# A hybrid block on one core: x and the first weights delivered by partition, x normalised in place behind the first projection

## The chip, the core and the metric

The kernel runs on one core of a Trainium2 chip, as one launch. The metric is the device time in microseconds (us); three runs of the kernel before took 1364.17, 1364.27 and 1365.17, the median is 1364.27.

The core has engines that work side by side, each through its own queue in order: TensorE (PE, with PEld for loading its stationary operand), VectorE (DVE), ScalarE (ACT), GpSimd (POOL), and SyncE (SP), which here only issues transfers (DMA). An instruction at the head of a queue that waits for a semaphore holds up all that stand behind it.

## The reference

The block has an RMS norm of x (512 tokens, 2048 features), one wide input projection, two mixers (a gated linear recurrence A, a sparse attention with an indexer B), gates, a merge, an output projection into the residual, and a final RMS norm. What matters here is its head:

```
h = rmsnorm(x, norm_w[layer])           # x / sqrt(mean(x^2) + 1e-6) * w, per token
proj = h @ w_in[layer]
(a_q, a_f, a_i, a_g, c_q, c_kv, k_idx_raw, w_idx_raw, b_g, m_a, m_b) = jnp.split(proj, SPLIT_POINTS, axis=-1)
...
cq = rmsnorm(c_q, q_norm_w)
k_idx = layernorm(k_idx_raw, kidx_norm_w, kidx_norm_b)
w_idx = w_idx_raw * (IDX_HEADS ** -0.5 * IDX_DIM ** -0.5)
```

The norm of x is a factor per token times a weight per feature. Since a projection is linear, the factor per token may be applied to h or to the columns of proj.

## The kernel before, in words

All large products are taken in three passes: each operand is split into a rounded high part (ACT copies it to a narrower format) and the low rest (DVE subtracts), and high x high, low x high and high x low are summed on TensorE. So `split` (L71) is one ACT and one DVE instruction, and every tile of weights costs both (`prep`, L157, fills two tiles ahead; `load`, L123, has two raw buffers, so a load waits until the low part of the tile two before it is done).

`start` (L250) is the first stage. x comes in four blocks of 128 tokens, tokens on partitions. For each block ACT squares and sums (L299), the factor per token goes onto a diagonal (L307), TensorE transposes 16 pieces of 128 x 128 (L313) and spreads the factors over partitions by a product with ones (L339), DVE multiplies by weight and factor (L350, for the first block L318 and L399), ACT takes the high part (L322) and DVE or POOL the low part (L326). The results are xh and xl, features on partitions, 16 feature tiles of 512 tokens, which every later projection reads. In between, `project` (L371) multiplies each block by the first 272 columns (256 of a_i, 16 of w_idx): 48 matmuls of 272 columns a block, 192 in all. The small vectors come as rows and are turned by one transposition (L432).

Behind it the order is that of the list `jobs` at the end: `feat_job` for kidx (L1167, 48 matmuls of 512 columns), two for cq (L1169, L1171) and one for ckv (L1173), 96 each, and then the pairs (`pair_unit`, L1096), which multiply 2 x 2 blocks of features and tokens with seven products in place of eight. The pairs need sums and differences of x: `pair_gen` (L1057) forms x again as xh + xl (L1061), takes four differences of 256 tokens (L1064 to L1067) and splits them. Such generators stand in lanes and are moved on one step by `pump` (L189), which `feat_job` calls after each column tile of each chunk of four feature tiles; `prep` comes once per chunk. The step at which a lane starts thus sets which of its instructions stand next to each other and which have a weight split between them. `kidx_gen` (L602) normalises the keys in lane "norm": two splits, two pairs of matmuls with ones (L609), one row of factors by Ln and Exp.

Of the kernel before, what the change touches and what calls it, by code (L numbers as in the profile page):

```python
# [50 lines left out]
def hybrid_block(ctx, tc, x, norm_w, w_in, lb_table, gnorm_a, q_norm_w, kv_norm_w, w_uq,  # L51
                 w_qidx, w_ukv, kidx_norm_w, kidx_norm_b, w_pa, w_pb, w_out, rel_bias,
                 final_norm_w, c_ident, c_levels, c_buckets, c_flip, out):
# [38 lines left out]
    const.tile([128, 16], F32, name="gap")  # L92
# [156 lines left out]

    def start():  # L250
        R.v0 = enter("v0")
        p0 = enter("p0", side="right")
        ident = p0.tile([128, 128], F32, name="ident")
        A.dma_start(ident, c_ident)
        HF = D // 2
        nw = p0.tile([16, 128], F32, name="nw")
        wc = p0.tile([128, 16], F32, name="wc")
        xs = [[p0.tile([128, HF], F32, name=f"x{t}{i}") for i in range(2)] for t in range(4)]
        ys = [p0.tile([128, 4, 128], F32, name=f"y{g}") for g in range(4)]
        diag = p0.tile([128, 128], F32, name="diag")  # L260
        sq = p0.tile([128, HF], mybir.dt.bfloat16, name="sq")
        st = p0.tile([128, 4, 4], F32, name="st")
        rows = p0.tile([128, 128], F32, name="rows")
        G.memset(rows, 1.0)
        G.tensor_copy(ones_r, rows)
        wh = [p0.tile([128, 4, 272], FR, name=f"fh{i}") for i in range(4)]
        wl = [p0.tile([128, 4, 272], FR, name=f"fl{i}") for i in range(4)]
        raw = [None] * 4

        def load_x(t):  # L270
            for i in range(2):
                SP.dma_start(xs[t][i], x2[t * 128:(t + 1) * 128, i * HF:(i + 1) * HF])

        def load_w(i):
            raw[i] = p0.tile([128, 4, 272], F32, name=f"fr{i}")
            for o, c0, c1 in ((0, 2048, 2304), (256, 4992, 5008)):
                SP.dma_start(raw[i][:, :, o:o + c1 - c0],
                             w_in[i * 512:(i + 1) * 512, c0:c1].rearrange("(k p) n -> p k n", p=128))

        SP.dma_start(nw, norm_w.rearrange("o (k d) -> (o k) d", d=128))  # L280
        load_x(0)
        load_w(0)
        load_w(1)
        load_x(1)
        load_w(2)
        load_w(3)
        load_x(2)
        load_x(3)
        A.activation(st[:, 0, 0:1], eps, AF.Sqrt)
        warm = bank("warm")  # L290
        for _ in range(4):
            PE.matmul(warm[:, 0:128], ones, ones, start=True, stop=True)
        G.memset(rows, 0.0)
        pw = mmp.tile([128, T], F32, name="acc")
        PE.transpose(pw[:, 0:16], nw, ident[0:16, 0:16])
        V.tensor_copy(wc, pw[:, 0:16])

        def square(t, i):
            A.activation(sq, xs[t][i], AF.Square, accum_out=st[:, t, i:i + 1])  # L299

        def rstd(t):
            V.tensor_add(st[:, t, 2:3], st[:, t, 0:1], st[:, t, 1:2])
            A.activation(st[:, t, 2:3], st[:, t, 2:3], AF.Sqrt, bias=eps, scale=1.0 / D)

        def on_diag(t):
            V.reciprocal(st[:, t, 3:4], st[:, t, 2:3])
            V.tensor_scalar(diag, ident, st[:, t, 3:4], None, op0=OP.mult)  # L307

        def turn(t, g):
            pt = bank("pt")  # L310
            for j in range(4):
                k = g * 4 + j
                PE.transpose(pt[:, j * 128:(j + 1) * 128],  # L313
                             xs[t][k // 8][:, (k % 8) * 128:(k % 8) * 128 + 128], ident)
            return pt

        def weigh(pt, g):
            V.tensor_tensor(ys[g], pt.rearrange("p (j t) -> p j t", j=4),  # L318
                            wc[:, g * 4:g * 4 + 4, None].to_broadcast([128, 4, 128]), op=OP.mult)

        def high(t, g):
            A.activation(xh[g][:, :, t * 128:t * 128 + 128], ys[g], AF.Copy)  # L322

        def low(t, g):
            o = slice(t * 128, t * 128 + 128)
            (G if t and g % 2 else V).tensor_tensor(xl[g][:, :, o], ys[g], xh[g][:, :, o].bitcast(F32),  # L326
                                                    op=OP.subtract)

        def w_high(i):
            A.activation(wh[i], raw[i], AF.Copy)  # L330

        def w_low(i, eng):
            eng.tensor_tensor(wl[i], raw[i], wh[i].bitcast(F32), op=OP.subtract)

        v = hg[0, "v"] = R.v0.tile([128, 4, 256], F32, name="hv")

        def spread():
            pr = mmp.tile([128, T], F32, name="acc")
            PE.matmul(pr[:, 0:128], ones, diag, start=True, stop=True)  # L339
            r = p0.tile([128, 128], F32, name="rrow", bufs=2)  # L340
            V.tensor_copy(r, pr[:, 0:128])
            return r
# [1231 lines left out]
```

## Time and profile before

| | |
|---|---|
| profiled execution | 1364.6 us |
| its span, first to last instruction | 1362.5 us |
| mean granted TensorE clock | 0.997 |
| instructions | 26714 |
| read from HBM | 167.89 MB, 149 GB/s with what is written |
| DMA engines, mean busy share, 47 to 125 us | 0.46 |

The profile is one execution. Its page gives busy time by engine and the chain of work that ended last, followed back from the end. The queries of the trace give groups of instructions (line, engine, operation, output <- input, shapes, count, busy time, mean duration in ns, idle time of the engine ahead of them and its releaser), timelines (start, duration, engine, line; in brackets the idle time before and its releaser), waits (line <- releaser: us in total, times, longest), and windows (busy time of each engine in a stretch, then granted clock, DMA share and GB/s).

### The profile page before, as it was taken

Reading aid. Unit: us, or ns where it says so; the run is one execution under the profiler, and the core shown is the slowest. Engines: PE = TensorE matmul, PEld = TensorE weight load, DVE = VectorE, ACT = ScalarE, POOL = GpSimd, SP = SyncE. Lnnn points to the kernel's source line nnn. Section 1 sums busy time; section 2 is a strip of 40 time slices with the busy share of each in tenths; the row PEclk is TensorE's granted clock in tenths of the full one; section 3 lists DMA queues with packets and bytes.
Section 4 is the critical chain, followed back from the end, with each engine's and each line's share of the span. In section 5 each row is a group of like instructions: output and inputs, shape, how many; then the busy total and the mean of one; then the engine's idle time right before and its main releaser. Section 6 shows DMA issues by size and latency. Waiting matters only on the chain.

```text
span 1362.5 us, 26714 instructions
## 1 busy us (share of the span) xinstructions
PE 1345.9 (99%) x10940; PEld 1250.4 (92%) x10940; DVE 1065.8 (78%) x1744; ACT 654.7 (48%) x1047; POOL 42.0 (3%) x57
## 2 busy tenths in 40 slices
PE   7999999999999999999999999999999999999997
PEld 7888999999999999999999798888888888899996
DVE  7896889998898888886777888775556658899856
ACT  5555445445554445445655353546434334354434
POOL 2100000000000000000000000020101100000000
PEclk9999999999999999999999999999999999999999
DMA  6334345544453454445334433435856556643554
GB/s 207 94 108 140 96 154 157 158 149 139 128 148 109 135 152 144 147 144 164 104 104 125 140 86 117 128 114 185 267 163 204 192 179 216 209 153 112 171 198 172
DMA packets 144156, 204.77 MB, mean 150 GB/s; under 512 B 10473, under 2 KB 85922, under 8 KB 143906
## 3 DMA queue, kind: packets, MB, share of 16 engines
q1 hardware_dynamic: 143746, 202.75, 47.6%
q8 instruction: 85, 1.39, 0.4%
q10 hardware_dynamic: 288, 0.33, 0.1%
q14 instruction: 37, 0.30, 0.1%
HBM read 167.89 MB, written 35.15 MB: 149 GB/s over the span
## 4 chain that ended last, share of the span: by engine, by line
PE 94%; DVE 3%; ACT 1%; issue 1%; DMA 0%; SPq 0%; ACTq 0%; DVEq 0%
PE pp L78 15%; PE pp L77 15%; PE pp L76 15%; PE acc L76 13%; PE acc L78 13%; PE acc L77 13%; PE hl L81 2%; PE acc L81 1%; PE ho L81 1%; PE sc L76 1%; PE sc L77 1%; PE sc L78 1%; PE pt L313 0%; PE hp L81 0%; PE po L78 0%
## 5 line engine op out<-in xcount | busy, mean ns | idle before, releaser
L150 ACT ACTIVATE bh<-wr 128x768 fp32r<-128x768 f32 x128 | 108.1, 845 | 218.3 <-issue 110.7
L152 ACT ACTIVATE wh<-sv 128x512 fp32r<-128x512 f32 x256 | 151.6, 622 | 85.6 <-DVE sv L145 66.5
L73 DVE TENSOR_TENSOR wl<-wr,wh 128x1024 fp32r<-128x1024 f32 (+1 forms) x104 | 125.7, 1209 | 61.5 <-ACT wh L72 61.2
L78 PE MATMUL pp<-sh,wl 128*128 128x256 f32 x624 | 172.8, 277 | 0.0
L76 PE MATMUL pp<-sh,wh 128*128 128x256 f32 x624 | 172.8, 277 | 0.0
L77 PE MATMUL pp<-sl,wh 128*128 128x256 f32 x624 | 172.7, 277 | 0.0
L153 DVE TENSOR_TENSOR bl<-wr,bh 128x768 fp32r<-128x768 f32 x128 | 122.3, 955 | 51.3 <-ACT bh L150 50.7
L154 DVE TENSOR_TENSOR wl<-sv,wh 128x1024 fp32r<-128x1024 f32 x128 | 156.5, 1223 | 7.3 <-ACT wh L152 1.1
L72 ACT ACTIVATE wh<-wr 128x1024 fp32r<-128x1024 f32 (+1 forms) x104 | 108.1, 1041 | 109.3 <-PE acc L77 57.5
L76 PE MATMUL acc<-xh,wh 128*128 128x512 f32 x304 | 121.4, 399 | 0.0
L78 PE MATMUL acc<-xh,wl 128*128 128x512 f32 x304 | 118.7, 390 | 0.0
L77 PE MATMUL acc<-xl,wh 128*128 128x512 f32 x304 | 118.5, 390 | 0.0
L77 PEld LDWEIGHTS pp<-sl,wh 128*128 128x128 f32 x624 | 117.4, 188 | 0.0
L78 PEld LDWEIGHTS pp<-sh,wl 128*128 128x128 f32 x624 | 117.3, 188 | 0.0
L76 PEld LDWEIGHTS pp<-sh,wh 128*128 128x128 f32 x624 | 117.3, 188 | 0.0
L78 PE MATMUL pp<-xh,bl 128*128 128x256 f32 x416 | 114.9, 276 | 0.0
L77 PE MATMUL pp<-xl,bh 128*128 128x256 f32 x416 | 114.9, 276 | 0.0
L76 PE MATMUL pp<-xh,bh 128*128 128x256 f32 x416 | 114.9, 276 | 0.0
L76 PE MATMUL acc<-yh,wh 128*128 128x512 f32 x256 | 100.2, 392 | 0.0
L78 PE MATMUL acc<-yh,wl 128*128 128x512 f32 x256 | 99.8, 390 | 0.0
L77 PE MATMUL acc<-yl,wh 128*128 128x512 f32 x256 | 99.8, 390 | 0.0
L145 DVE TENSOR_TENSOR sv<-wr 128x512 f32<-128x512 f32 x128 | 87.9, 687 | 8.5 <-DMA wr<-in_w_in_dram 6.5
(395 smaller groups left out, 3638.7 us busy)
## 6 DMA issues: line engine op xcount, KB each, us to landing
wr<-in_w_in_dram SPq DMA_DIRECT2D x136, 512.0 KB, 3.7
wr<-in_w_out_dram SPq DMA_DIRECT2D x32, 512.0 KB, 3.7
mg<-gate_d SPq DMA_DIRECT2D x48, 256.0 KB, 4.2
gate_d<-c SPq DMA_DIRECT2D x44, 256.0 KB, 5.1
wr<-in_w_in_dram SPq DMA_DIRECT2D x36, 256.0 KB, 3.0
wr<-in_w_pa_dram SPq DMA_DIRECT2D x16, 512.0 KB, 6.0
wr<-in_w_pb_dram SPq DMA_DIRECT2D x16, 512.0 KB, 4.7
x<-in_x_dram SPq DMA_DIRECT2D x8, 512.0 KB, 4.8
```

Source lines behind the costliest of these rows:

```text
L72: A.activation(hi, src, AF.Copy)
L73: V.tensor_tensor(lo, src, hi.bitcast(F32), op=OP.subtract)
L76: PE.matmul(ps, lh, rh, start=first, stop=False, skip_group_check=True)
L77: PE.matmul(ps, lh, rl, start=False, stop=False, skip_group_check=True)
L78: PE.matmul(ps, ll, rh, start=False, stop=last, skip_group_check=True)
L81: PE.matmul(ps, l, r, start=first, stop=last, skip_group_check=True)
L145: V.tensor_tensor(sv[:, 0:2, :], b[:, 1:3, :], b[:, 0:1, :].to_broadcast([128, 2, 256]), op=OP.add)
L150: A.activation(bh, b[:, 1:4, :], AF.Copy)
L152: A.activation(vh[:, i:i + 2, :], sv[:, i:i + 2, :], AF.Copy)
L153: V.tensor_tensor(bl, b[:, 1:4, :], bh.bitcast(F32), op=OP.subtract)
L154: V.tensor_tensor(vl, sv, vh.bitcast(F32), op=OP.subtract)
```

## The change

- The host lays out x with features on partitions (x_t), the 272 first weight columns by partition (w_first), norm_w (w_norm), and the small vectors as columns (w_cols). No transposition is left in the first stage, and no L313, L339, L350.
- The first projection takes high and low parts of x times norm_w, without the factor per token, all four token blocks together, in five chunks of 2, 2, 4, 4, 4 feature tiles. ACT takes the high parts (scale by norm_w), DVE the low parts, POOL the high parts of the weights. ACT squares x by pairs of tiles into two buffers, DVE sums them (`add`, one chunk late).
- The factor is formed behind the first chunk of kidx (`stats`), the first projection's results are scaled by it there, and it is spread over partitions behind the second (`spread`). kidx and the first cq job run on x without factor, and their evacuations (now on DVE) multiply by it.
- x is normalised in place on DVE (`normal`) behind kidx and in the first cq job, where xh and xl are also split anew (`renew`). `pair_gen` reads this x, without the addition, and enters its lane after the first cq job in place of before kidx.

```diff
-            A.activation(xh[g][:, :, t * 128:t * 128 + 128], ys[g], AF.Copy)
...
+        parts = ((0, 2), (2, 4), (4, 8), (8, 12), (12, 16))
...
+        def square(k):
+            squares[k] = p0.tile([128, 2, T], F32, name="sq", bufs=2)
+            A.activation(squares[k], R.xt[k], AF.Square)
+
+        def add(k):
+            if k:
+                V.tensor_tensor(sums, squares.pop(0) if k == 1 else sums, squares.pop(k), op=OP.add)
...
+        for c, (k0, k1) in enumerate(parts):
+            n = slice(0, k1 - k0)
+            wh.append(p0.tile([128, 4, 272], FR, name="fh", bufs=3))
+            wl.append(p0.tile([128, 4, 272], FR, name="fl", bufs=3))
+            G.tensor_copy(wh[c][:, n], wr[c][:, n])
+            for k in range(k0, k1):
+                src = R.xt[k // 2][:, k % 2, :]
+                hi, lo = xh[k // 4][:, k % 4, :], xl[k // 4][:, k % 4, :]
+                A.activation(hi, src, AF.Copy, scale=wc[:, k:k + 1])
+                V.scalar_tensor_tensor(lo, src, wc[:, k:k + 1], hi.bitcast(F32), op0=OP.mult, op1=OP.subtract)
+            V.tensor_tensor(wl[c][:, n], wr[c][:, n], wh[c][:, n].bitcast(F32), op=OP.subtract)
+            if c < 2:
+                load_group(c + 3)
+            while behind:
+                add(behind.popleft())
+            for k in range(k0 // 2, k1 // 2):
+                square(k)
+                behind.append(k)
+            for n in range(3):
+                three(c, n)
+        load_ahead()
+        while behind:
+            add(behind.popleft())
+        V.tensor_tensor(R.total, sums[:, 0, :], sums[:, 1, :], op=OP.add)
...
+    def stats():
+        ps = bank("st")
+        for t in range(4):
+            PE.matmul(ps[:, t:t + 1], R.total[:, t * 128:t * 128 + 128], ones[:, 0:1], start=True, stop=True)
+        A.activation(R.rinv, ps[:, 0:4], AF.Sqrt, bias=eps, scale=1.0 / D)
+        V.reciprocal(R.rinv, R.rinv)
...
+    def spread():
+        ps = bank("st")
+        PE.matmul(ps, ones, R.dg[:, 128:640], start=True, stop=True)
+        A.activation(R.row, ps, AF.Copy)
+
+    def normal(k):
+        for i in range(2):
+            y = R.xt[k][:, i, :]
+            V.scalar_tensor_tensor(y, y, wc[:, 2 * k + i:2 * k + i + 1], R.row, op0=OP.mult, op1=OP.mult)
+
+    def renew(k):
+        s = slice(2 * (k % 2), 2 * (k % 2) + 2)
+        split(xh[k // 2][:, s, :], xl[k // 2][:, s, :], R.xt[k])
...
-        A.activation(R.kx[:, 0, :], ps, AF.Copy)
+        V.tensor_tensor(R.kx[:, 0, :], ps, R.row, op=OP.mult)
...
-            V.tensor_tensor(a, xh[k // 2][:, s, :].bitcast(F32), xl[k // 2][:, s, :].bitcast(F32), op=OP.add)
...
+    feat_job(w_in, 4864, 1, NK, 4, x_rhs, kx_evac,
+             after={0: stats, 1: spread, 2: lambda: normal(0), 3: lambda: (normal(1), normal(2))})
+    lane("norm", kidx_gen)
+    feat_job(w_in, 4096, 2, NK, 4, x_rhs, cq_evac(0),
+             after={i: lambda i=i: ([renew(k) for k in (2 * i, 2 * i + 1)],
+                                    [normal(k) for k in ((3,), (4, 5), (6, 7), ())[i]]) for i in range(4)})
     lane("misc", pair_gen)
-    feat_job(w_in, 4864, 1, NK, 4, x_rhs, kx_evac)
-    lane("norm", kidx_gen)
-    feat_job(w_in, 4096, 2, NK, 4, x_rhs, cq_evac(0))
```

How the instructions now stand is shown at three places. Lines in rows of the changed kernel are its own.

First, ACT in the first projection: xh are the high parts, sq the squares (two buffers in turn, each read by DVE's sums), wh the high parts of kidx's weights. Before, from its second block of tokens on:

```order
L299 ACTIVATE sq_123,st_124<-x20_114 128x1024
L322 ACTIVATE xh2_90<-y2_120 128x4x128
L299 ACTIVATE sq_123,st_124<-x21_115 128x1024
L322 ACTIVATE xh2_90<-y3_121 128x4x128
L303 ACTIVATE st_124<-st_124,cols_75 128x1
```

and in the changed kernel, from chunk 2 (feature tiles 4 to 7) to kidx:

```order
L332 ACTIVATE xh1_92<-xt2_114,wc_80 128x512 x2
L332 ACTIVATE xh1_92<-xt3_117,wc_80 128x512 x2
L309 ACTIVATE sq_248<-xt2_114 128x1024
L309 ACTIVATE sq_250<-xt3_117 128x1024
L332 ACTIVATE xh2_90<-xt4_119,wc_80 128x512 x2
L332 ACTIVATE xh2_90<-xt5_121,wc_80 128x512 x2
L309 ACTIVATE sq_314<-xt4_119 128x1024
L309 ACTIVATE sq_316<-xt5_121 128x1024
L332 ACTIVATE xh2_90<-xt6_123,wc_80 128x512 x2
L332 ACTIVATE xh2_90<-xt7_125,wc_80 128x512 x2
```

Before, a square wrote a scratch tile that nobody reads and a sum beside it; now each pair of squares stands between the high parts of one chunk and those of the next, and writes a buffer that DVE must have read.

Second, DVE in `pair_gen`: sv are the differences, sl the low part of a pair's sums (it needs the high part sh, which ACT makes from sv), wl the low part of weights. Before:

```order
L1061 TENSOR_TENSOR sv_880<-xh2_90,xl2_93 128x1024
L1064 TENSOR_TENSOR sv_882<-sv_880 128x256
L1065 TENSOR_TENSOR sv_882<-sv_880 128x256
L1066 TENSOR_TENSOR sv_882<-sv_882,sv_880 128x256
L1067 TENSOR_TENSOR sv_882<-sv_882,sv_880 128x256
L73 TENSOR_TENSOR wl_888<-wr_805,wh_887 128x1024
L73 TENSOR_TENSOR sl4_907<-sv_882,sh4_906 128x1024
```

and in the changed kernel:

```order
L1005 TENSOR_TENSOR sv_819<-xt1_111 128x256
L1006 TENSOR_TENSOR sv_819<-xt1_111 128x256
L1007 TENSOR_TENSOR sv_819<-sv_819,xt1_111 128x256
L1008 TENSOR_TENSOR sv_819<-sv_819,xt1_111 128x256
L72 TENSOR_TENSOR sl1_112<-sv_819,sh1_836 128x1024
L72 TENSOR_TENSOR wl_840<-wr_772,wh_839 128x1024
```

The addition is gone, and the weight subtract that stood between the last difference and sl now stands behind sl.

Third, DVE from the middle of the first cq job on, where before there were only weights, key normalisation and pairs (nt and suml belong to the key normalisation, L622 and L605 before):

```order
L72 TENSOR_TENSOR suml_646<-nsq_619,sumh_645 128x512
L72 TENSOR_TENSOR xl1_95<-xt2_114,xh1_92 128x1024
L72 TENSOR_TENSOR xl1_95<-xt3_117,xh1_92 128x1024
L374 SCALAR_TENSOR_TENSOR xt4_119<-xt4_119,wc_80,dg6_124 128x512 x2
L374 SCALAR_TENSOR_TENSOR xt5_121<-xt5_121,wc_80,dg6_124 128x512 x2
L72 TENSOR_TENSOR wl_676<-wr_596,wh_675 128x1024
L569 SCALAR_TENSOR_TENSOR nt_617<-nt_617,cols_75,rr_664 128x512
```

The renewed low parts (xl) and the normalisations (xt, with the spread factor dg6) stand among the weights and the steps of the key normalisation, in one queue.

More of the change, by code (lines that the diff above doesn't have):

```diff
@@ L248, in x_rhs @@
         return xh[k // 4][:, k % 4, :], xl[k // 4][:, k % 4, :]
+    xs_h, xs_l = [], []
     def start():
         R.v0 = enter("v0")
+        R.x = enter("sums")
         p0 = enter("p0", side="right")
[L253 to L280, printed above, removed]
@@ L282, in start @@
+        A.dma_start(wc, w_norm)
+        load_x(0, 0)
         load_w(0)
+        load_x(0, 1)
         load_w(1)
         load_x(1)
[L285 to L291, printed above, removed]
-            PE.matmul(warm[:, 0:128], ones, ones, start=True, stop=True)
-        G.memset(rows, 0.0)
-        pw = mmp.tile([128, T], F32, name="acc")
-        PE.transpose(pw[:, 0:16], nw, ident[0:16, 0:16])
@@ L296, in start @@
[L296 to L333, printed above, removed]
-        v = hg[0, "v"] = R.v0.tile([128, 4, 256], F32, name="hv")
[L337 to L342, printed above, removed]
@@ L387, in start @@
-        pts = [turn(0, g) for g in range(4)]
-        weigh(pts[0], 0)
-        weigh(pts[1], 1)
-        square(0, 0)
-        square(0, 1)
-        rstd(0)
-        on_diag(0)
-        w_high(0)
-        weigh(pts[2], 2)
-        r = spread()
-        def scaled(g):
-            V.tensor_tensor(ys[g], ys[g], r[:, None, :].to_broadcast([128, 4, 128]), op=OP.mult)
-            high(0, g)
-        scaled(0)
-        scaled(1)
-        w_low(0, V)
-        w_high(1)
-        low(0, 0)
-        weigh(pts[3], 3)
@@ new lines, in start @@
+        load_group(2)
+        heat_src = p0.tile([128, 128], F32, name="rows")
+        G.memset(heat_src, 1.0)
+        G.tensor_copy(ones_r, heat_src)
+        A.activation(R.rinv[:, 0:1], eps, AF.Sqrt)
+        warm = mmp.tile([128, T], F32, name="acc")
+        for _ in range(8):
+            PE.matmul(warm[:, 0:128], ones, ones, start=True, stop=True)
+        pools4 = [(mmp, "acc"), (sdp, "sd")] * 2
+        accs = [pool.tile([128, T], F32, name="pf", tag=tag)[:, 0:272] for pool, tag in pools4]
@@ L1042, in open_norms @@
         R.kx = R.i.tile([128, 1, T], F32, name="kx")
-        R.x = enter("sums")
     def open_pairs():
```

147 lines of the change are left out of this document (66 added, 81 removed).

## The prediction

> **What bounds the kernel now.** I read the page first, then who waited for whom on TensorE, then the timelines of TensorE, VectorE (DVE) and ScalarE (ACT) over the first 130 us, where the whole change lies.
>
> ```profile
> PE 1345.9 (99%) x10940; PEld 1250.4 (92%) x10940; DVE 1065.8 (78%) x1744; ACT 654.7 (48%) x1047; POOL 42.0 (3%) x57
> PE 94%; DVE 3%; ACT 1%; issue 1%; DMA 0%; SPq 0%; ACTq 0%; DVEq 0%
> ```
>
> TensorE bounds it: it is busy 99% of the span and 94% of the last chain. Its waits, longest first (line, waited for, us, times):
>
> ```profile
> PE pt L313 <- DMA x<-in_x_dram: 2.3, 1, 2.3
> PE acc L81 <- ACT xh L322: 1.8, 1, 1.8
> ...
> PE hl L81 <- DVE tot L789: 0.5, 1, 0.5
> ```
>
> All but some 1.2 us of its waiting lies before 38 us. Behind that, any wait that the change brings is added to the end whole, and any work that it removes comes off whole. TensorE's timeline (start, us, what):
>
> ```profile
> 5.99 3.68 PE L313 MATMUL pt<-ident,x 128*128 128x128 f32 x16 [2.32 <-DMA x<-in_x_dram]
> 24.41 0.66 PE L81 MATMUL acc<-fh,xh 128*128 128x272 f32 x4
> 26.91 0.67 PE L81 MATMUL acc<-fl,xh 128*128 128x272 f32 x4
> 47.11 0.48 PE L76 MATMUL acc<-xh,wh 128*128 128x512 f32 x1
> 49.28 0.39 PE L76 MATMUL acc<-xh,wh 128*128 128x512 f32 x1
> 58.12 0.39 PE L76 MATMUL acc<-xh,wh 128*128 128x512 f32 x1
> 125.23 0.28 PE L76 MATMUL pp<-xh,bh 128*128 128x256 f32 x1
> ```
>
> Three marks matter: the first real work at 5.99, the first kidx matmul at 47.11 (end of the first projection), the first matmul of the pairs at 125.23. From 24.41 to 26.91 five groups of four go by, 0.125 us a matmul, so the 192 of the first projection are 24.0 us; the other 23 are loads, transpositions, the spreading of norm factors and waits. From 49.28 to 58.12 are 39 matmuls of 512 columns, 0.227 each.
>
> **The first projection after the change.** It loses 64 transpositions and the waits around them, and keeps the 192 matmuls. Rows for what feeds it (chain of waits; groups of instructions; windows with, at the end, granted clock, DMA share and GB/s):
>
> ```profile
> 1.19 4.76 DMA x<-in_x_dram
> L448 POOL CAST levels<-lev 128x192 uint8<-128x192 f32 x1 | 0.3, 342 | 585.7 <-DMA lev<-in_levels_dram 585.7
> L265 POOL CAST ones_r<-rows 128x128 fp32r<-128x128 f32 x1 | 0.3, 289 | 0.1
> L333 POOL TENSOR_TENSOR fl<-fr,fh 128x1088 fp32r<-128x1088 f32 x1 | 2.5, 2542 | 19.6 <-ACT fh L330 19.6
> L299 ACT ACTIVATE sq<-x 128x1024 bf16<-128x1024 f32 x8 | 8.4, 1045 | 3.5 <-DMA x<-in_x_dram 3.4
> L333 DVE TENSOR_TENSOR fl<-fr,fh 128x1088 fp32r<-128x1088 f32 x3 | 3.9, 1288 | 0.5 <-ACT fh L330 0.5
> L622 DVE SCALAR_TENSOR_TENSOR nt<-nt,cols,rr 128x512 f32<-128x512 f32 x1 | 0.7, 747 | 0.0
> L1487 ACT ACTIVATE o<-o,rfin x4: 722/724/725, 1345.7 to 1356.8; 128x512 f32<-128x512 f32 x4
> 8.00:10.00 2.00, 2.00 (x10) 1.61 (x8) 1.60 (x5) 1.67 (x4) 0.00 (x0) 1.00 1.15 355
> 10.00:12.00 2.00, 0.27 (x2) 0.08 (x1) 1.86 (x5) 0.80 (x3) 0.00 (x0) 1.00 1.02 394
> 12.00:14.00 2.00, 0.98 (x5) 0.77 (x6) 2.00 (x3) 2.00 (x3) 0.00 (x0) 0.84 1.14 338
> 14.00:16.00 2.00, 2.00 (x10) 2.00 (x11) 2.00 (x4) 1.26 (x3) 0.00 (x0) 0.50 1.17 343
> 16.00:18.00 2.00, 2.00 (x13) 1.78 (x13) 1.50 (x3) 1.83 (x3) 0.00 (x0) 0.80 1.04 412
> ```
>
> Start: the first x load took 4.76 us to land; half of it, issued 0.4 us earlier, lands at about 5.7, the first weights behind it at 6.4. POOL's cast of the weights is not in the trace at this size: two casts give 0.83 ns an element, 0.63 us for 544, its subtract 2.3 ns, 1.3 us; I take the cast, first matmul at 7.2 (7.9 by the other). Chunks 0 and 1 have 24 matmuls (3.0 us) each, chunk 2 has 48 (6.0): TensorE is through them at 19.5.
>
> Then a loop binds. There are two square buffers; the next square (ACT) needs the sum (DVE) that stands behind the chunk's weight subtract, and the next chunk's x copies stand behind the squares in ACT's queue. One turn: copy 0.72, four x subtracts of the L622 kind (0.75, next one 0.67 later) 2.68, weight subtract 1.21, sum 1.22, two squares 2.0, handing over 0.3: 8.1 us against 6.0 of TensorE. Chunk 2's last x lands at 13.7 (3.2 MB ahead of it at 0.36 MB/us), so its squares end at 20.3 and chunk 3 starts at 21.0, chunk 4 at 29.1, and kidx, whose weight copy stands behind chunk 4's squares, at 37.3. Against 47.11 that is **9.8 us gained**. Without the loop it would be 7.2 + 24.0 = 31.4, 15.7 gained; with slow casts and loads 39, 8 gained.
>
> **From kidx to the pairs.** Here work is added to DVE. Its timeline before (start, us), the windows row of the stretch, and rows for what it waits on:
>
> ```profile
> 47.11:125.23 78.12, 78.12 (x345) 64.14 (x343) 62.24 (x94) 42.90 (x55) 0.00 (x0) 1.00 0.46 132
> 54.25 0.42 DVE L1064 TENSOR_TENSOR sv<-sv 128x256 f32<-128x256 f32 x1
> 54.59 0.42 DVE L1065 TENSOR_TENSOR sv<-sv 128x256 f32<-128x256 f32 x1
> 54.92 0.42 DVE L1066 TENSOR_TENSOR sv<-sv 128x256 f32<-128x256 f32 x1
> 55.38 0.42 DVE L1067 TENSOR_TENSOR sv<-sv 128x256 f32<-128x256 f32 x1
> 55.72 1.22 DVE L73 TENSOR_TENSOR wl<-wr,wh 128x1024 fp32r<-128x1024 f32 x1
> 56.93 1.23 DVE L73 TENSOR_TENSOR sl<-sv,sh 128x1024 fp32r<-128x1024 f32 x1
> 58.07 1.22 DVE L73 TENSOR_TENSOR wl<-wr,wh 128x1024 fp32r<-128x1024 f32 x1
> 63.07 0.68 DVE L73 TENSOR_TENSOR suml<-kx,sumh 128x512 fp32r<-128x512 f32 x1
> 63.67 1.22 DVE L73 TENSOR_TENSOR sl<-sv,sh 128x1024 fp32r<-128x1024 f32 x1
> L504 ACT ACT_TABLE_LOAD x1 | 1.3, 1283 | 0.0
> wr<-in_w_in_dram SPq DMA_DIRECT2D x4, 256.0 KB, 3.0
> ```
>
> Before, DVE is busy 62 of 78 us and TensorE never waits. An operation frees DVE 0.08 us before its end: 1024 wide 1.14, 512 wide 0.60, 256 wide 0.34.
>
> The change drops eight additions (L1061, 9 us) and adds sixteen normalisations (16 x 0.67 = 10.7), eight renewed low parts (8 x 1.14 = 9.1), three evacuations (1.8), the diagonal (0.6), and the sums that are still queued when kidx starts. In the changed order DVE's last sum ends at 38.2, the total at 38.8; from there to the low half of the first pair's weights (wl) I count 29 operations of 1024 (33.1 us), 18 of the L622 kind (12.1), 15 of 512 (9.0), 34 of 256 (11.9), and small ones (3.1): 69.2 us of work.
>
> Its waits, as I find them by laying the rows of all queues end to end with these spacings (the order of before, laid out in the same way, gives 47.0 and 124.6 for the marks at 47.11 and 125.23):
> - Pairs: before, a weight subtract stood between the four differences and the pair's low part (55.72 above) and covered ACT's rounding (1.06 and two handovers). Now they stand next to each other: 8 x 1.24, and once more 0.6, 10.5 us.
> - Weights: only two raw buffers, so kidx's third load starts when wl of the first is done: 3.0 to land and 0.6 to cast, 3.2 us seen by DVE; the next ones, 2.9.
> - Row constants: two table loads of 1.28 stand in ACT's queue before the square root, 1.2.
> - The key normalisation and the renewals hold each other up: ACT waits in its queue for TensorE's sums, which wait for DVE's low part, while the renewed high parts wait behind on ACT: 1.8, 4.0 and three under 1, 7.6 in all.
> - Handovers between dependent instructions and the query sums: 3.7.
>
> Together 29.1. DVE ends wl at 38.8 + 69.2 + 29.1 = 137.1; in the laid-out rows, with the handovers, 137.7.
>
> TensorE's own work in the stretch is 336 x 0.227 = 76.2 us, the key and query sums 1.9 (78.1 less 76.2), and the new sums and spread 2.0: 80.1, so it would be there at 117.4. DVE is 20 us late. TensorE pays for it in pieces: 1.7 on kidx's first low half, 1.9 on the diagonal, 1.1 and 2.5 on the key sums, 2.4 at the third projection, 3.9 on the query sums, 5.7 at the first pair. There it comes to its third matmul at 137.7, which before was at 125.23 + 0.23: 12.2 later, and about 1 more when it waits for the second pair's weights. **Sum: 13 us slower**, 9.8 gained and some 23 given back. The other edits cost nothing on the path: the four evacuations of the first projection move behind the statistics, where their banks are not needed until cq, and the small columns come by DMA beside the big loads in place of one transposition.
>
> **Rivals.**
> - *Faster.* DVE keeps up between kidx and the pairs, because its waits overlap. Work alone ends at 38.8 + 69.2 = 108, before TensorE's 117.4. The point is how much DVE waits: at 29 us the loss is 13, at 16 nothing is lost, at 9 TensorE is the bound and the time is 9.8 less the 2.0 of new matmuls better, 1356.5. For it: that TensorE never waited for DVE here before. Against it: the pair waits alone are 10.5 and stand in the order. Chance 0.09.
> - *Nothing to be seen* (within 0.2%, 2.7 us, about what a measurement can tell from no change): DVE waits 13 to 19. Chance 0.04.
> - *Slower still: the clock.* In the windows above TensorE stood mostly idle from 10 to 13.4, and its granted clock fell to half for 3.4 us (0.84, 0.50, 0.80), which cost 1.7 of work. The 3.0 and 2.7 that I expect around the first pair lie together and could do that, as could the 3.9 on the query sums: up to 1.7 each where DVE does not bind, and with DVE spacings 3% longer (2.5 more) 1382. Chance 0.10. The Trainium skill, TensorE: Matmul & The Clock Gate, Part 1, says that the clock is halved after an idle window of about 3.4 us and comes back after a busy one of the same length; the trace agrees, with 3.4 us at half after such an idle stretch, and the rule would put the time near 1379.
> - *The change does not shorten the start*: POOL casts at 2.3 ns an element. They take 2.5 of each 8.1 us, beside the loop. It stays in the range.
>
> **Numbers.** The profiled execution took 1364.6 (span 1362.5), the median is 1364.27. 1364.6 + 13 = 1377.6, from the median 1377.3. The forecast, slower by 7 to 17, has 0.77. The range goes from 1368, where a third of DVE's waits are covered, to 1382. Faster 0.09, same 0.04, slower 0.87.
>
> **What would show it.** First kidx matmul near 37; ACT waiting over 3 us for DVE's sums before each of the squares of chunks 2 to 4; DVE waiting about 1.2 us for each of eight sh; DVE busy nearly all the time from 75 to 137 but for those; TensorE waiting for DVE and ACT some 20 us between 37 and 140 and for nothing later; the first pair at 133 to 138. I am wrong if TensorE reaches it before 125, or if it waits in the first projection for loads and not for ACT.

## The result, and the profile after

The changed kernel took 1381.4 us (median of 1379.86, 1381.24, 1381.56 and 1382.56) against 1364.2 of the kernel before (1363.69 to 1365.17): a ratio of 1.0124, 95% interval 1.0107 to 1.0142, 17.2 us slower. The prediction was 1377.3, from 1368 to 1382. The profiled execution took 1379.9, its span is 1378.0 (before 1362.5), so the trace accounts for 15.5 of the 17.2.

The page of the changed kernel, busy times and the chain that ended last, and TensorE's waits over the whole span (line, waited for, us, times, longest):

```profile
PE 1349.5 (98%) x10884; PEld 1249.2 (91%) x10884; DVE 1072.0 (78%) x1707; ACT 660.0 (48%) x1039; POOL 38.4 (3%) x54
PE 84%; DVE 7%; ACT 4%; DMA 2%; issue 2%; SPq 0%; DVEq 0%; ACTq 0%
```

```profile
PE pf L80 <- ACT xh L332: 3.3, 2, 2.0
PE ns L80 <- DVE suml L72: 3.1, 2, 2.2
PE ns L80 <- ACT sumh L71: 2.7, 1, 2.7
PE pp L77 <- DVE bl L152: 2.4, 1, 2.4
PE acc L77 <- DVE wl L72: 2.0, 2, 1.6
PE hl L80 <- issue: 1.6, 1, 1.6
...
PE t L80 <- DMA bf<-t_d: 1.2, 1, 1.2
PE st L368 <- DVE dg L359: 0.9, 1, 0.9
PE acc L75 <- issue: 0.5, 1, 0.5
```

TensorE still does nearly the same work, but where the chain was its own to 94%, DVE now holds 7% of it. All the waits above but three are of the stretch that the change touches; the two on "issue" and the one on t_d come near 704, 753 and 771 us, in code that the change does not touch.

TensorE's timeline (start, us, what, idle time before it) at the marks of the prediction:

```profile
5.32 2.04 PE L80 MATMUL pf<-fh,xh 128*128 128x272 f32 x8 [0.16 <-POOL fh L328]
20.09 2.52 PE L80 MATMUL pf<-fh,xh 128*128 128x272 f32 x16 [1.32 <-ACT xh L332]
29.09 3.32 PE L80 MATMUL pf<-fh,xh 128*128 128x272 f32 x16 [1.97 <-ACT xh L332]
37.04 0.50 PE L75 MATMUL acc<-xh,wh 128*128 128x512 f32 x1
136.44 0.58 PE L77 MATMUL pp<-xh,bl 128*128 128x256 f32 x1 [2.42 <-DVE bl L152]
139.36 0.28 PE L75 MATMUL pp<-sh,wh 128*128 128x256 f32 x1
```

kidx starts 10.1 sooner than before (37.04 against 47.11), and the third pair matmul 11.0 later (136.44 against 125.23 + 0.23). From there to the end of the span it is 1241.6 (1378.0 - 136.44); before it was 1237.0 (1362.5 - 125.46). So 21.0 were given back ahead of the pairs (10.1 and 11.0, before rounding), and 4.5 more were lost behind that mark. 1.4 of the 4.5 are seen at once: thirteen matmuls from 136.44 to 139.36 took 2.92, where the kernel before has 0.118 each, 1.53. The granted clock (before the DMA share, at the end of a row) had dropped:

```profile
114.00:118.00 4.00, 1.98 (x4) 1.36 (x5) 3.17 (x7) 0.63 (x1) 0.00 (x0) 0.68 0.69 188
118.00:122.00 4.00, 4.00 (x10) 3.11 (x10) 2.88 (x5) 3.78 (x4) 0.00 (x0) 0.50 0.02 8
134.00:138.00 4.00, 1.58 (x8) 1.56 (x8) 3.93 (x6) 1.99 (x3) 0.00 (x0) 0.74 0.11 12
138.00:142.00 4.00, 4.00 (x32) 4.00 (x32) 3.90 (x7) 3.29 (x6) 0.00 (x0) 0.84 0.57 144
```

What DVE waited for from kidx to the pairs (groups of its instructions: count, busy us, mean ns, idle us before them and who ended it), and its busy time in that stretch (in the windows row TensorE's busy time comes first, then that of its weight loads, then DVE's):

```profile
L72 DVE TENSOR_TENSOR wl<-wr,wh 128x1024 fp32r<-128x1024 f32 (+1 forms) x16 | 17.3, 1086 | 6.5 <-ACT wh L71 6.5
L72 DVE TENSOR_TENSOR sl<-sv,sh 128x1024 fp32r<-128x1024 f32 x8 | 9.8, 1226 | 9.9 <-ACT sh L71 9.9
L72 DVE TENSOR_TENSOR xl<-xt,xh 128x1024 fp32r<-128x1024 f32 x8 | 9.4, 1220 | 6.2 <-ACT xh L71 6.2
```

```profile
37.00:136.40 99.40, 88.16 (x354) 69.65 (x354) 72.47 (x113) 50.62 (x64) 0.00 (x0) 0.93 0.32 90
```

DVE is idle for 27 of 99 us, and 22.6 of them stand in these three groups: the pairs 9.9, the loads of weights 6.5, the renewals 6.2. TensorE is busy for 88.2 of them at a granted clock of 0.93, and waits 11.2.

### The profile page after: what moved, and what is told of

The parts are those of the page before. It is cut to its first block, busy times and chain, and to the rows that moved or that the text cites. A ratio compares the mean times of both kernels' runs of the same rounds, so it can differ in the third digit from the quotient of the medians.

```text
span 1378.0 us, 26558 instructions
## 1 busy us (share of the span) xinstructions
PE 1349.5 (98%) x10884; PEld 1249.2 (91%) x10884; DVE 1072.0 (78%) x1707; ACT 660.0 (48%) x1039; POOL 38.4 (3%) x54
## 3 DMA queue, kind: packets, MB, share of 16 engines
q8 instruction: 85, 1.39, 0.4%
## 4 chain that ended last, share of the span: by engine, by line
PE 84%; DVE 7%; ACT 4%; DMA 2%; issue 2%; SPq 0%; DVEq 0%; ACTq 0%
PE pp L75 15%; PE pp L77 15%; PE pp L76 15%; PE acc L75 11%; PE acc L77 11%; PE acc L76 10%; PE hl L80 1%; DVE wl L72 1%; PE ho L80 1%; DVE xt L374 1%; DVE sums L313 1%; DMA wr<-in_w_qidx_dram 1%; DVE xl L333 1%; DMA wr<-in_w_in_dram 1%; ACT sh L71 1%
```

## The experiments

My theory: from the end of the first projection to the pairs DVE's queue decides, by its work and by waits that stand between its instructions; the larger part of them came with the late and tight pairs. The rivals: the order does not matter and only the added work does; or TensorE's clock, halved after idle stretches, is what is lost. Each kernel below is timed beside the kernel before, whose medians in the three sittings were 1364.0, 1364.1 and 1364.1.

**The late pairs alone, in the kernel before.**

```diff
     lane("misc", lb_gen)
-    lane("misc", pair_gen)
     feat_job(w_in, 4864, 1, NK, 4, x_rhs, kx_evac)
     lane("norm", kidx_gen)
     feat_job(w_in, 4096, 2, NK, 4, x_rhs, cq_evac(0))
+    lane("misc", pair_gen)
```

> The kernel before with one part of the change: the pair generator enters its lane behind the first cq job in place of before kidx (its additions stay, nothing else is changed). My theory: the differences and the low part of each pair then stand next to each other on DVE, each pair waits about 1.2 us for ACT's rounding, and all eight fall into the last two jobs before the pairs; the rows laid end to end give the third pair matmul 11.6 us later than before and TensorE waits of 1 to 2 at the query sums, 7 and 3 at the first pair. Time 1376, 10 to 13 slower than before. Rival A (it is the added work, normalisations and renewals, that makes DVE late; DVE has 16 us of slack here before): 1364, no change. Rival B (the clock after idle stretches makes the loss): no waits, no change either, 1364.

Measured: 1377.0, 13.0 slower (1.0092, 1.0078 to 1.0106). TensorE's timeline at the pairs:

```profile
132.69 0.58 PE L76 MATMUL pp<-xh,bh 128*128 128x256 f32 x1 [6.77 <-ACT bh L150]
...
135.60 0.58 PE L78 MATMUL pp<-xh,bl 128*128 128x256 f32 x1 [2.12 <-DVE bl L153]
```

DVE's group of low parts of the pairs, in the kernel before and then here:

```profile
L73 DVE TENSOR_TENSOR sl<-sv,sh 128x1024 fp32r<-128x1024 f32 x8 | 9.8, 1223 | 0.3 <-ACT sh L72 0.3
L73 DVE TENSOR_TENSOR sl<-sv,sh 128x1024 fp32r<-128x1024 f32 x8 | 9.8, 1225 | 9.0 <-ACT sh L72 9.0
```

The third pair matmul is 10.1 later than in the kernel before (135.60 against 125.47), and DVE waits 8.7 more for the pairs' high parts. The place of one line in the list of jobs costs the old kernel, which has none of the new work, 13.0, where the whole change cost 17.2. Of the 21.0 that the changed kernel gave back ahead of the pairs, these 10.1 are about half; the other half, the added work and the waits that it brings, was not run alone. Rival A falls for this part: there is slack in DVE's 78 us as a whole, and none in the two jobs into which the pairs are now put.

**A weight subtract between the pairs' halves again.**

```diff
     def pair_gen():
+        yield
         for k in range(8):
```

> The changed kernel with one more step ahead of the first pair, so that a weight subtract stands between the differences and the low part of each pair again. My theory: most of the eight waits of 1.13 us on DVE go; what the last pair gains is taken in part by its handing over to the first pair's weights, so the rows laid end to end give the third pair matmul 4.3 us sooner, 132, and no wait at the query sums: 1377 against 1381.4 of the changed kernel. Rival A (DVE's work alone binds, waits of it lie beside other waits): within 1 us of 1381.4. Rival B (the clock): the waits of 2.7 and 2.2 us before the pairs go, and two windows at half clock with them, 3.4: 1378, so this run separates A from the others only.

Measured: 1378.9 (runs 1376.4, 1376.8, 1381.0, 1381.0); the profiled execution is one of the two long ones. The group of low parts in it:

```profile
L72 DVE TENSOR_TENSOR sl<-sv,sh 128x1024 fp32r<-128x1024 f32 x8 | 9.8, 1225 | 7.4 <-ACT sh L71 7.4
```

Only 2.5 of the 9.9 went, and the third pair matmul came at 134.05, 2.4 sooner. Three of the eight wait for nothing or 0.26; two wait 1.24 and 2.56 for ACT although a weight subtract stands there, and the last three follow each other ahead of the pairs' own weights with none between them, 1.13 each. Half of what I expected, and by the time alone not told apart from nothing.

**The sums ahead of the low parts.**

```diff
             G.tensor_copy(wh[c][:, n], wr[c][:, n])
+            while behind:
+                add(behind.popleft())
             for k in range(k0, k1):
...
-            while behind:
-                add(behind.popleft())
```

> The changed kernel with the sums of the squares ahead of the next chunk's low parts in DVE's queue, so that ACT's next squares no longer wait for a weight subtract. My theory: the loop of 8.1 us a chunk falls to 6.2 (two sums 2.3, four low parts 2.7, weights 1.2), kidx starts near 32 in place of 37.0, and as DVE has its sums behind it sooner too, the third pair matmul comes 5.6 sooner, near 131: 1376. Rival A (what binds from kidx on is a queue on DVE and ACT that does not begin with the first projection): kidx at 32, but the pairs at 136 as in the changed kernel, 1381. Rival B (loads bind the first projection, not the loop): kidx at 36 to 37, 1381.

Measured: 1376.9 (1.0098, 1.0085 to 1.0112). ACT's waits ahead of the squares, its timeline:

```profile
19.35 1.06 ACT L309 ACTIVATE sq<-xt 128x1024 f32<-128x1024 f32 x1 [1.12 <-DVE sums L313]
...
26.50 1.06 ACT L309 ACTIVATE sq<-xt 128x1024 f32<-128x1024 f32 x1 [2.31 <-DVE sums L313]
```

In the changed kernel these waits, ahead of the squares of chunks 2, 3 and 4, were 3.48, 4.23 and 3.36. The first is gone, the others fell to 1.1 and 2.3, and kidx starts at 33.82 in place of 37.04, and the third pair matmul at 132.84 in place of 136.44. The 3.2 gained at the start arrive at the pairs whole, since DVE too was through its sums sooner: the loop was the limit of the first projection, and DVE the limit behind it.

**The renewed low parts on POOL.**

```diff
-        split(xh[k // 2][:, s, :], xl[k // 2][:, s, :], R.xt[k])
+        A.activation(hi, R.xt[k], AF.Copy)
+        G.tensor_tensor(lo, R.xt[k], hi.bitcast(F32), op=OP.subtract)
```

> The changed kernel with the eight renewed low parts on POOL in place of DVE; POOL does nothing after 24 us otherwise. My theory (DVE binds from kidx to the pairs): DVE is rid of 8 times 1.14 = 9.1 us; POOL takes 2.3 ns an element, 2.4 us each. Third pair matmul 9.2 us sooner, near 127: 1372. Rival A (the waits between ACT, DVE and TensorE bind, not DVE's work): under 3 us sooner, 1379 to 1381. Rival B (POOL and DVE hinder each other, or TensorE then waits for POOL's low parts): DVE's subtracts beside POOL's become longer than 1.2 us, gain under 5, 1377 or more.

Measured: 1384.8 (1.0159, 1.0145 to 1.0173), 3.4 slower than the changed kernel. POOL's timeline, then DVE's, then DVE's groups of normalisations and of two steps of the key normalisation from 60 to 95 us:

```profile
82.55 8.17 POOL L380 TENSOR_TENSOR xl<-xt,xh 128x1024 fp32r<-128x1024 f32 x3 [2.76 <-ACT xh L379]
```

```profile
82.16 9.11 DVE L374 SCALAR_TENSOR_TENSOR xt<-xt,wc,dg 128x512 f32<-128x512 f32 x4
92.32 1.28 DVE L465 TENSOR_TENSOR cq<-acc,dg 128x512 f32<-128x512 f32 x2
```

```profile
L374 DVE SCALAR_TENSOR_TENSOR xt<-xt,wc,dg 128x512 f32<-128x512 f32 x10 | 13.2, 1380 | 0.0
L571 DVE SCALAR_TENSOR_TENSOR nt<-nt,cols,rr 128x512 f32<-128x512 f32 x1 | 2.9, 2873 | 0.0
L72 DVE TENSOR_TENSOR suml<-nsq,sumh 128x512 fp32r<-128x512 f32 x1 | 2.8, 2826 | 0.0
```

Four normalisations that take 2.73 alone took 9.11 beside three subtracts on POOL. In this stretch DVE's ten normalisations took 13.2 in place of 6.9, the key sums' low part 2.8 and the key step nt 2.9 in place of 0.7 each, and four weight subtracts 7.0 in place of 4.9. That is some 12.6 more, against the 9.4 of low parts that were taken from it, and the third pair matmul comes at 139.34, 2.9 later. This is rival B. The two operations at 92.32 read one of their inputs from TensorE's accumulator; POOL subtracts from 92.49 on, and they take the 1.28 that they take in the changed kernel. The Trainium skill, SBUF — State Buffer, section "SBUF: two separate sides", says that a DVE operation with two inputs from that memory and a POOL operation that reads it share a pair of ports, and whichever starts first holds it for its whole instruction. The trace agrees: suml and nt end 2.1 late, somewhat less than POOL's subtract of 2.39 alone.

**The same place in TensorE's instruction stream.** The changed kernel has 10884 matmuls, the one before 10940.

```diff
             PE.matmul(warm[:, 0:128], ones, ones, start=True, stop=True)
+        for _ in range(56):
+            mm(warm[0:32, 0:32], ones_r[:, 0:32], ones_r[:, 0:32], True, True)
```

> The changed kernel with 56 tiny matmuls (32 columns, results unused) behind the warm-up, so that TensorE has the 10940 matmuls of the kernel before again and everything from the pairs on stands at the same place of its instruction stream as there. It is for the 2.8 us that are lost behind the pairs: in the kernel before and in late_pairs_before TensorE waits there 0.5, 0.4 and 0.3, in all runs with the changed start 0.5 to 0.8, 0.7 to 1.2 (on a DMA) and 1.5 to 1.8 (on nothing the profile shows). Theory S (the waits on nothing belong to fixed places of TensorE's instruction stream, and fall into the run of tiny matmuls of the recurrence since 56 matmuls are gone): the waits of 0.5 and 1.6 near 700 and 770 go, one of 0.3 near 830 comes as before, 2 less: 1379. Rival T (they belong to the state of the transfers there or to this part of the program): the wait of 1.6 stays at its place, 1381. The start is 0.7 to 1.4 later in TensorE's queue, which its wait ahead of chunk 3 covers; third pair matmul at 136.4 in both.

Measured: 1376.4 (1.0091, 1.0077 to 1.0105), 5.0 less than the changed kernel. In the changed kernel the three late waits, and the page's row of the queue that brings instructions (packets, MB, share):

```profile
704.13 0.28 PE L75 MATMUL acc<-wh,xh 128*128 128x256 f32 x1 [0.52 <-issue]
...
753.12 0.51 PE L80 MATMUL t<-bf,flip 128*128 128x512 f32 x1 [1.16 <-DMA bf<-t_d]
...
771.25 0.45 PE L80 MATMUL hl<-hqk 128*32 128x32 f32 x29 [1.58 <-issue]
```

```profile
q8 instruction: 85, 1.39, 0.4%
```

and all waits of over 0.1 us behind 140 us with the 56 matmuls:

```profile
718.65 0.70 PE L80 MATMUL hl<-hqk 128*32 128x32 f32 x32 [0.54 <-DVE tot L738]
766.37 0.76 PE L80 MATMUL hl<-hqk 128*32 128x32 f32 x64 [0.38 <-DVE hqk L736]
```

All three are gone, the one on a transfer too, and from the third pair matmul (135.05) to the end it is 1238.8 in place of 1241.6. That mark itself came 1.4 sooner, which neither theory says; 0.5 of it is there when kidx starts (36.50). 1.39 MB in 85 packets is 16 KB each, and a matmul with its weight load takes 1.39 MB / 10884 = 128 bytes, so one packet holds 128 matmuls (with 166 more, in waits_filled below, the row has 86 packets and 1.41 MB), and 56 move the bounds of the packets by nearly half of one. In the changed kernel one packet is under way from 768 to 769 us, and the wait of 1.58 begins at 769.7, among matmuls that take 0.011 us each. A window from 0 to a wait counts the matmuls ahead of it, here to the last of the three:

```profile
0.00:771.24 771.24, 750.73 (x6353) 722.91 (x6353) 633.13 (x944) 392.56 (x608) 9.50 (x17) 0.99 0.45 137
```

In all six kernels with the changed start and without padding the two waits on "issue" stand behind 5461 and behind 6352 or 6353 matmuls, 892 apart, which is nearly seven times 128, though their times differ by up to 16 us. The small wait on "issue" of the kernel before (0.33 at 815.70) stands behind 7117, and 764 more is nearly six times 128. So theory S holds: the place in the stream decides. That TensorE waits there for a packet is what it looks like; what delays it was not tried.

**TensorE kept busy in its waits.**

```diff
+    def heat(ps, n):
+        for _ in range(n):
+            mm(ps[:, 0:128], ones_r, ones_r, True, True)
```

with n of 16 and 24 ahead of chunks 3 and 4, 20 ahead of kidx, 10 and 28 ahead of the key sums, 36 ahead of the query sums and 32 ahead of the first pair.

> The changed kernel with 166 matmuls of 128 columns on ones (results overwritten) in TensorE's queue at the places of its seven longest waits before the pairs, in number no longer than the waits, so that its clock is not halved there. In the changed kernel about 10 us of TensorE's work are lost to windows at half clock, 1.7 each. My theory (DVE binds from kidx to the pairs, so a faster TensorE waits longer): half windows gone, third pair matmul at 136.4 within 0.7, and only the window behind it, where TensorE is at work, pays, 1.4: 1380. Rival (the clock is what is lost): five to six windows of 1.7, of which at least three on the path: third pair matmul before 133, 1376 or less.

Measured: 1376.1 (1.0087, 1.0073 to 1.0101). The granted clock of the execution is 0.999 (0.991 in the changed kernel), and the third pair matmul still waits for DVE:

```profile
135.22 0.39 PE L77 MATMUL pp<-xh,bl 128*128 128x256 f32 x1 [1.18 <-DVE bl L156]
```

By the time alone this would be the rival's number. But the 166 matmuls also move the stream, and the late waits are gone here as in stream_shift. Against that run, which kept all the half clocks (0.62 from 40 to 44, 0.68 from 136 to 140), the pairs come 0.2 later and the time is 0.4 less. The comparison is not a clean one: the 20 matmuls ahead of kidx take 2.2 us and fill no wait, so kidx starts at 38.78 in place of 36.50. But at the third projection TensorE waits 2.00 for DVE in this run and 2.03 in that one, and goes on at 87.73 and 87.57. Up to there neither the full clock nor the late start made a difference, and at the pairs it waits for DVE again: full clock ahead of the pairs is worth nothing where DVE sets the mark.

**The pairs earlier**, with three idle steps ahead of the first.

```diff
     lane("norm", kidx_gen)
+    lane("misc", pair_gen)
     feat_job(w_in, 4096, 2, NK, 4, x_rhs, cq_evac(0),
...
-    lane("misc", pair_gen)
```

> The changed kernel with the pair generator entered ahead of the first cq job with three idle steps, so that it starts 5 steps sooner and a weight subtract stands between differences and low part. My theory (the late, tight pairs are the larger part of what was given back, as late_pairs_before shows for the old kernel): the last pair's low part is done before the last chunks, no wait of 2.4 at the first pair, the waits move forward to the third projection (5 and 2); third pair matmul at 131, 5.5 sooner, and no half clock behind it: 1375. Rival A (weights_between gained only 2.4 at that mark, so DVE's work binds and order matters little): 134 or later, 1379. Rival B (the pairs ahead of cq's weights hold up the third projection by as much as is gained): no change, 1381.

Measured: 1374.5 (1.0075, 1.0062 to 1.0089), 6.9 less than the changed kernel.

```profile
91.71 0.50 PE L77 MATMUL acc<-xh,wl 128*128 128x512 f32 x1 [3.25 <-DVE wl L72]
98.92 0.50 PE L77 MATMUL acc<-xh,wl 128*128 128x512 f32 x1 [1.43 <-DVE wl L72]
...
131.94 0.28 PE L77 MATMUL pp<-xh,bl 128*128 128x256 f32 x1
```

```profile
L72 DVE TENSOR_TENSOR sl<-sv,sh 128x1024 fp32r<-128x1024 f32 x8 | 9.8, 1222 | 2.5 <-ACT sh L71 2.5
```

Much as the theory has it: DVE's waits for the pairs fell from 9.9 to 2.5, and TensorE is 4.5 sooner at that mark (5.5 expected), with no wait at the pairs, waits of 3.25 and 1.43 at the third projection in their place, and no half clock behind. The late waits are still there (0.9, 0.8 and 1.9).

**Three edits together**: sums_first, the pairs ahead of the first cq job with five idle steps, and `lane("norm", kidx_gen)` moved from ahead of the first cq job to behind it.

> Three edits together: sums ahead of the low parts (as sums_first), the key normalisation behind the first cq job in place of before it, the pair generator ahead of the first cq job with five idle steps. My theory: the rows laid end to end give the third pair matmul 16 us sooner than in the changed kernel; sums_first came to 3.6 of its 5.6, so I take 14: 122.5, 3 sooner than the kernel before, which the 2.8 lost behind the pairs take back: 1364 to 1366, the same as before. Rival A (the gains overlap, since each takes out the same wait of DVE): 127 to 130, 1370 to 1373. Rival B (TensorE's own work binds already): 117, 1358.

Measured: 1369.2 (1.0038, 1.0026 to 1.0051), 12.2 less than the changed kernel. The third pair matmul came at 124.41, 12.0 sooner than in the changed kernel where I took 14, so A and B fall; it is 1.1 sooner than in the kernel before. Alone, the sums gave 3.6 and the early pairs 4.5; the move of the keys was not run alone, so what it gave is not shown. The time is 4 more than I took: roughly 1.9 lie ahead of that mark, and 2.7 behind it, where this run lost 5.5 against the kernel before in place of the 2.8 that I had. It has waits of 0.71, 0.91 and 2.12 there, the last one followed by ten us at 0.83 of the clock.

**The same, with the 56 matmuls** ahead of the second of the two key sums.

> sums_keys_pairs with 56 tiny matmuls (32 columns, results overwritten) ahead of the key sums, where TensorE waited 5.0 us, so that from there on every matmul has the number in TensorE's stream that it had in the kernel before. sums_keys_pairs reached the pairs at 124.41, 1.1 sooner than the kernel before, and lost 5.5 behind them: waits of 0.7, 0.9 and 2.1 and a window at half clock. Theory S (place in TensorE's instruction stream): these go, 1369.2 less 5.4 is 1364, the same as before. Rival T (it is the state of transfers or of the program there): 1369.

Measured: 1367.3 (1.0021, 1.0012 to 1.0030); the profiled execution took 1364.7 and the other ten 1365.2 to 1368.4. TensorE's timeline at the key sums:

```profile
82.30 0.79 PE L80 MATMUL ns<-suml,ones_r 128*128 128x512 f32 x1 [4.97 <-DVE suml L72]
90.02 1.92 PE L80 MATMUL ns<-ones_r 128*32 128x32 f32 x56
91.78 0.48 PE L80 MATMUL ns<-sumh,ones_r 128*128 128x512 f32 x1
```

The wait of 5.0 stands at the first key sum and the 56 matmuls ahead of the second, where TensorE waits for nothing: they do not fill the wait, as was meant, but cost 1.8 us here and in the three kernels below. The late waits are gone, 1237.1 from the third pair matmul to the end as in the kernel before, and that mark is 1.3 later (125.69). The theory holds for the profiled execution; what the others lost is not seen.

**kidx's weights split in the first projection**, on top of combined_stream.

```diff
+            if c == 2:
+                load_ahead()
+            if c == 4:
+                prep(-1)
...
-        load_ahead()
```

> combined_stream, and kidx's first two weight tiles are loaded and split inside the first projection (in its chunks 2 and 4), so that the third raw tile can be loaded sooner; in sums_keys_pairs DVE waited 4.4 us for it. My theory (DVE binds up to the pairs, every wait taken from it comes off until TensorE's own work binds): DVE's wait of 4.4 goes, the rows laid end to end give the pairs 3.1 sooner, at 121.3: 1361, 3 faster than before. Rival A (that wait lies beside others, above all ahead of the key sums): 1364.

Measured: 1363.0 (0.9993, 0.9984 to 1.0002), no difference from the kernel before. The third pair matmul came at 122.79, 2.9 sooner than in combined_stream: the theory's 3.1. The mark is thus 1.5 later than the 121.3 expected, because combined_stream's own came later than I had it, and the time 2 above the 1361.

**The casts of the first weights on ACT.**

```diff
-            G.tensor_copy(wh[c][:, n], wr[c][:, n])
+            if c < 2:
+                G.tensor_copy(wh[c][:, n], wr[c][:, n])
+            else:
+                A.activation(wh[c][:, n], wr[c][:, n], AF.Copy)
```

> weights_first with the casts of the first weights of chunks 2 to 4 on ACT in place of POOL. In sums_first DVE's four low parts of a chunk took 3.56 where POOL cast and 2.73 where it did not, and in low_on_pool DVE's normalisations took up to 2.7 each beside POOL's subtracts. Theory P (an operation of POOL makes DVE's longer): DVE gets back 0.84 a chunk, the first projection ends 1 to 2 sooner than in weights_first, near 32, and the time is 1 to 2 lower. Rival (ACT's three casts of 1.1 hold up its high parts by more): the rows laid end to end, which know nothing of POOL hindering DVE, give kidx 0.6 later, time the same or 0.6 higher.

Measured: 1360.8 (0.9975, 0.9966 to 0.9984). DVE's low parts of chunk 2 in weights_first, and then here:

```profile
13.01 3.57 DVE L335 SCALAR_TENSOR_TENSOR xl<-xt,wc,xh 128x512 fp32r<-128x512 f32 x4
```

```profile
12.44 2.74 DVE L338 SCALAR_TENSOR_TENSOR xl<-xt,wc,xh 128x512 fp32r<-128x512 f32 x4 [0.47 <-ACT xh L337]
```

Theory P: kidx starts at 31.19 in place of 33.33, and the time is 2.2 less. In the profiled executions, though, the third pair matmul is only 0.8 sooner (121.97). From the wait of 4.97 at the key sums to the pairs TensorE waits for nothing in either, and its half clock after that wait covers 5.1 us of its work here (78.1 to 83.2) and 2.8 in weights_first (80.0 to 82.8), which is 1.2 us of time. So the clock does cost where TensorE itself sets the mark. This kernel is 3.3 us faster than the one before and 20.6 faster than the changed one.

**The keys early again.** casts_on_act with the key normalisation back ahead of the first cq job, one more idle step in it, three idle steps ahead of the pairs.

> casts_on_act with the key normalisation ahead of the first cq job again as in the changed kernel, one more idle step between its splits and its sums, and three idle steps ahead of the first pair in place of five. The rows laid end to end give the pairs 1.8 sooner than casts_on_act and the last wait at the third projection (3.4) in place of 5.4 at the key sums. My theory: near 119.5 for the pairs, 1.5 lower than casts_on_act, 1358 to 1359, where TensorE's own work (31.5 + 80.1 + 0.8) would be at 112.4. Rival (keys and renewals interlock on ACT again, as the 7.6 of the prediction says): 2 to 4 higher than casts_on_act.

Measured: 1360.5 (0.9974, 0.9964 to 0.9985), the same as casts_on_act. The profiled execution, the fastest of eight at 1358.1, has one wait left from kidx to the pairs:

```profile
84.43 0.50 PE L77 MATMUL acc<-xh,wl 128*128 128x512 f32 x1 [3.15 <-DVE wl L72]
```

and its third pair matmul at 119.12, 2.9 sooner than casts_on_act. The rival falls; that the medians do not follow the mark is open.

## Why the prediction was right, and where it was not

Right: the direction, the place and the mechanism. Point by point, forecast and measured:

| | forecast | measured |
|---|---|---|
| first real work | 7.2 | 5.32 |
| chunk 3, chunk 4 of the first projection | 21.0, 29.1 | 20.09, 29.09 |
| first kidx matmul | 37.3 | 37.04 |
| ACT's waits ahead of the squares of chunks 2, 3, 4 | over 3 each | 3.5, 4.2, 3.4 |
| DVE's work, 38.8 to the pairs | 69.2 | 70.7 |
| DVE's waits there | 29.1 | 26.9 |
| DVE's pair waits | 10.5 | 9.9 |
| DVE's weight waits (third load, next ones) | 3.2 + 2.9 | 6.5 |
| renewals and key normalisation | 7.6 | 6.2 + 0.6 + 0.7 |
| table loads | 1.2 | 0.6 + 0.8 |
| handovers and query sums | 3.7 | 1.6 (what is left) |
| TensorE's own work, kidx to the pairs | 80.1 | 88.2 |
| TensorE waiting there | some 20 | 11.2 |
| third pair matmul | 137.7, 12.2 later | 136.44, 11.0 later |
| behind it | about 1 | 4.5 |
| sum, against the profiled execution | 13 | 15.3 |

The first projection came out by two errors that cancel, which is luck. The start is 1.9 sooner than I took (POOL's cast of 544 elements took 0.64, as estimated, and the first loads landed sooner), of which 0.9 is left at chunk 3, and a turn of the loop took 9.0 and then 7.95 where I had 8.1 for both: the four low parts of the first of the two stood beside a POOL cast and took 3.61 in place of 2.74. I had POOL's work "beside the loop"; casts_on_act shows that it was in it.

From kidx to the pairs DVE's sum was right nearly term by term; only the handovers came to less than half. Its largest term is shown by late_pairs_before from one side (0.3 of pair waits became 9.0, and the mark 10.1 later) and by pairs_early from the other (9.9 became 2.5, and the mark 4.5 sooner). DVE as the limit is shown by low_on_pool, where a slower DVE made the mark later, and by waits_filled, where TensorE at full clock waited for DVE at the same places and times as in stream_shift.

TensorE's side of that stretch was wrong, and it did not matter: I had it wait some 20 us, and it waited 11.2. Its clock was halved behind several of its waits (0.93 over the stretch, where it was 1.00 before), its work took 88.2 in place of 80.1, and this filled time in which it would have waited for DVE. The sum had no half clock at all; it came out because DVE and not TensorE set the mark. Two slips of arithmetic change nothing: 7.2 + 24.0 is 31.2, not 31.4, and 34 operations at 0.34 are 11.6, not 11.9.

Wrong is also that TensorE would wait for nothing later, and with it the size: I counted 1 behind the pairs, for a wait on the second pair's weights that did not come. There were 1.4 of half clock, and 3.9 of waits in place of the 1.2 of before, 3.3 of them near 704, 753 and 771. The first was in my rival but not in my sum: behind the wait of 2.42 the clock of 0.74 and 0.84 from 134 to 142 makes 3.4 us at half. The Trainium skill, TensorE: Matmul & The Clock Gate, Part 1, gives a window of about 3.4 us, idle for the drop and busy for the return. The trace agrees with the length of the half clock, but the idle stretch ahead of it was 2.4 and not 3.4. For the second I had no term: I took code that the change leaves alone for unchanged, though 56 matmuls fewer move every later one in its stream.

The rival "slower still: the clock" named the time nearly (1382), and for the wrong reason. Its half clocks did come, about 10 us of TensorE's work from 28 to 142, but stream_shift and waits_filled, with and without them, differ by 0.4, and ahead of the pairs they only took the place of waits for DVE. The rival "faster" had its condition right: with DVE's waits cut in casts_on_act the same new start is 3.3 faster than the kernel before.

Open: the 1.5 by which the median lies above the profiled execution, and the wider spread of all kernels with the new start (1379.9 to 1382.6, against 1363.7 to 1365.2). weights_between shows one way: there the late wait of 1.79 was followed by ten us at 0.83 of the clock, 1.7 lost, while in the changed kernel 1.58 was not. Another part is the start: in the four profiles whose first projection has the same instructions (changed kernel, weights_between, low_on_pool, pairs_early) kidx starts at 35.87 to 37.05, in the two with the old start at 46.77 and 47.11. Whether these make the whole spread was not tried. So differences of about 1 us between single profiles are no more than this spread, and the time differences of 2 and more, each from four or more executions, carry the argument.

## What to carry to other kernels

An engine with slack over a stretch can still be the limit of two jobs within it: count its work between the point where its inputs exist and the point where its results are due, and look which of its instructions wait for each other with nothing in between. A start that is 10 us shorter is worth only what the next limiting queue lets through; here the gain came out when DVE's waits were taken away one by one, most of them found by the idle time in front of a group. When instructions are taken out, expect waits to appear or go in untouched code behind them, and compare a kernel padded to the same place in the stream before a mechanism is blamed.

## What the runs showed of the hardware

- DVE operations with two inputs from SBUF took longer beside POOL's: 9.11 in place of 2.73 for four, beside three subtracts on POOL that took 8.17; 3.57 in place of 2.74 beside one cast. Two with an input from TensorE's accumulator took no longer (1.28).
- By the row of the instruction queue a packet goes with 128 matmuls and their weight loads. Among matmuls of 0.011 us, at the same matmul of the stream, a wait of 1.5 to 2.1 stood in six kernels with the changed start, and none in the eight whose stream was as before or padded. From the third pair matmul to the end the first six took 1241.6 to 1245.2, and the five with neither these waits, nor half clock there, nor the wait of 1.0 that waits_filled has at the pairs, 1237.0 to 1237.2.
- Keeping the clock up by filling TensorE's waits worked (0.999 granted), and paid nothing where another engine was the limit. The length of a wait did not decide alone: the clock fell to half behind the 1.58 at 39.35 in the changed kernel (0.57 from 40 to 44), and not behind the 3.25 at 91.71 in pairs_early (1.00 from 88 to 96).
